# An encoder kernel on one Trainium2 core: the triangular inverses of its RWKV chunks by substitution in blocks of 16 and small products

## The chip, the cores and the metric

The kernel runs on one core of one Trainium2 chip. The metric is the time of one execution in microseconds (us) on the device. The engines' names in the profile are PE (TensorE, matrix products), PEld (its weight loads), DVE (VectorE), ACT (ScalarE), POOL (GpSimd) and SP (SyncE, which here issues transfers).

## What is computed

Two requests of 512 and 256 rows go through two layers of width 1024. Layer 0 runs differential attention and a bidirectional RWKV-7 mixer side by side, layer 1 runs dilated attention, and each layer ends with a SwiGLU feed-forward part. The change touches the RWKV mixer alone, whose recurrence is, for each of 8 heads of width 64, once forward and once backward in time:

```python
def step(st, inp):
    r_t, w_t, k_t, v_t, kk_t, a_t = inp
    sa = jnp.einsum('bhvk,bhk->bhv', st, -kk_t)
    st = (st * w_t[:, :, None, :] + sa[..., None] * (kk_t * a_t)[:, :, None, :]
          + v_t[..., None] * k_t[:, :, None, :])
    y = jnp.einsum('bhvk,bhk->bhv', st, r_t)
    return st, y
...
y = (rwkv_scan(rh, heads(decay(w0_f, w1_f, w2_f)), heads(k_f), vh, kk, heads(a_f), False)
     + rwkv_scan(rh, heads(decay(w0_b, w1_b, w2_b)), heads(k_b), vh, kk, heads(a_b), True))
```

The kernel computes it in chunks of 64 rows. The rows of a chunk depend on one another through a triangular 64 x 64 matrix, one for each head, chunk and direction, and the kernel needs its inverse.

## The kernel before

The program has one long stage for each part of the network. What follows concerns the stretch from about 185 to 400 us, in which the operands of the RWKV mixer are made. Its loop runs over four steps j, one for each pair of heads; each step projects r, k and v (TensorE, tiles `gm`), and then does for the forward and the backward direction: `stage` (small products into `st` and `uv`, sigmoids `sw` and `sa` on ScalarE, L670), `operands` (a scan of `sw` on VectorE, exponentials `E` and `sw` on ScalarE, and passes of 768 columns on VectorE that make `kff` or `kfb`, `AL`, `RH`, `KB`, `KK`, L593 to L607), `store` (transfers), and `products` (64 x 64 products `pr<-AL,KB` on TensorE, L83, which ScalarE copies out of the accumulation banks in strips, L643 into `G`, L646 into `AO`). `G` collects the two 32 x 32 diagonal blocks of each chunk's matrix, `AO` the block off the diagonal. A group is 16 of the 48 pairs of chunk and step, with both heads and both directions on the 128 partitions in quarters of 32.

As soon as a group is full, `inverses` calls `invert` (L721): after step 1, 2 and 3 for group 0, 1 and 2. It transposes `G` into `M` (L728, L729), sets `X` to the identity, and finds the inverse of the 32 x 32 blocks by substitution, row by row, on VectorE:

```python
for i in range(1, 32):
    o = 0
    for k0, k1 in zip(KI, KI[1:]):
        if k0 < i:
            row(i, k0, min(i, k1), o)
        o += (31 - k0) * (k1 - k0)
```

A row is a product (L736) and a sum (L738), in two strips of columns (`KI`), 48 pairs for a group. Four transposes then bring the inverse into `M` and `tm` (L749, L750), twelve copies into `TS`, `Tif` and `Tib` (L768; eight on ScalarE, four on GpSimd), 64 products of 32 x 32 join the blocks over `AO` (`iv<-TS,AO`), a copy `Hs` (L773) and 64 more products follow (`iv<-Tif,Hs`, `iv<-Tib,Hs`), and ScalarE copies the result and issues its transfer to DRAM (L785). It is read only by the later RWKV stage, whose chain starts near 485 us.

The order of all instructions is planned when the program is built, by a scheduler that simulates the engines and takes the row with the best rank that is ready; products with `fp32r` operands, the `gm` rows, rank last and fill gaps. A change in one function so moves rows of others, and each engine then runs its rows in the planned order.

Of the kernel before, what the change touches and what calls it, by code (L numbers as in the profile page):

```python
# [8 lines left out]
F32 = mybir.dt.float32  # L9
# [4 lines left out]
ALU = mybir.AluOpType  # L14
AX = mybir.AxisListType
# [3 lines left out]
P = 128  # L19
# [11 lines left out]
NF = FH // P  # L31
SEQS = ((0, 512), (512, 256))
RT = 2
KI = (0, 14, 32)
SUBS = [lambda nc: nc.vector, lambda nc: nc.gpsimd] * 2
DUPS = [lambda nc: nc.scalar.copy] * 2
SPLIT = ((0, 512), (512, 256))
# [10 lines left out]
COLS, NCOL = {}, 0  # L48
# [5 lines left out]
class Core:  # L54
# [13 lines left out]

    def constants(self):
        for n, shp in (("ident", [P, P]), ("cols", [P, NCOL]), ("blk2", [P, 2]), ("nblk", [2, P])):  # L70
            t = self.const.tile(shp, F32, tag=n, name=n)
            self.nc.scalar.dma_start(t, self.A[n])
            setattr(self, n, t)

    def rank(self, n):

        return self.tc.high_priority(n)
# [643 lines left out]
    def invert(self, g, G, AO, park):  # L721

        nc = self.nc
        tile = lambda tag, shape: self.ip.tile(shape, F32, tag=tag, name=self.uid(tag), bufs=1)
        M, X, tm = tile("M", [P, 32, 32]), tile("X", [P, 32, 32]), tile("tm", [P, 32 * 32])
        nc.vector.transpose(out=M[0:64], in_=G[0:64])  # L728
        nc.vector.transpose(out=M[64:P, ::-1, ::-1], in_=G[64:P])  # L729
        nc.gpsimd.memset(X, 0.0)  # L730
        nc.gpsimd.memset(X.rearrange("p a b -> p (a b)")[:, ::33], 1.0)

        def row(i, k0, k1, o):
            n, w = k1 - k0, i - k0
            tv = tm[:, o:o + n * w].rearrange("p (a b) -> p a b", a=n)
            nc.vector.tensor_tensor(out=tv, in0=X[:, k0:k1, k0:i],  # L736
                                    in1=M[:, i, k0:i].unsqueeze(1).to_broadcast([P, n, w]), op=ALU.mult)
            nc.vector.tensor_reduce(out=X[:, k0:k1, i], in_=tv, axis=AX.X, op=ALU.add)  # L738
        for i in range(1, 32):

            o = 0
            for k0, k1 in zip(KI, KI[1:]):
                if k0 < i:
                    row(i, k0, min(i, k1), o)
                o += (31 - k0) * (k1 - k0)
        TN, TT = M, tm.rearrange("p (a b) -> p a b", a=32)
        for h, rv in ((slice(0, 64), False), (slice(64, P), True)):
            xv = X[h, ::-1, ::-1] if rv else X[h]
            nc.vector.transpose(out=TN[h], in_=xv)  # L749
            nc.vector.transpose(out=TT[h], in_=xv.rearrange("p j i -> p i j"))  # L750
        TS, Hs = tile("TS", [P, 16, 32]), tile("Hs", [P, 16, 32])
        Ti = [tile(n, [P, 16, 64]) for n in ("Tif", "Tib")]
        parts, copies = [], []
        for di in range(2):
            for par in range(2):
                q = 64 * di + 32 * par
                ba = di
                bb = 1 - ba
                ra, rb = (slice(64 * par + 32 * x, 64 * par + 32 * x + 32) for x in (ba, bb))
                tc = "p t c -> p c t"  # L760
                nc.gpsimd.memset(Ti[di][rb, :, 32 * ba:32 * ba + 32], 0.0)
                copies.append((TS[ra], TN[q:q + 32, :, 16 * ba:16 * ba + 16].rearrange(tc)))
                for x, rr in ((ba, ra), (bb, rb)):
                    copies.append((Ti[di][rr, :, 32 * x:32 * x + 32], TT[q:q + 32, :, 16 * x:16 * x + 16].rearrange(tc)))
                parts.append((di, ba, bb, ra, rb))

        for i, (o, x) in enumerate(copies):
            (nc.gpsimd.tensor_copy if i % 3 == 2 else nc.scalar.copy)(out=o, in_=x)  # L768
        hb = self.bank("iv")
        for c in range(16):  # L770
            for di, ba, bb, ra, rb in parts:
                self.mm(hb[rb, c * 32:c * 32 + 32], AO[ra, c], TS[ra, c])
        nc.scalar.copy(out=Hs.rearrange("p c t -> p (c t)"), in_=hb)  # L773
        hb = self.bank("iv")
        for c in range(16):
            for di, ba, bb, ra, rb in parts:
                self.mm(hb[ra, c * 32:c * 32 + 32], Hs[rb, c], Ti[di][rb, c, 32 * bb:32 * bb + 32])
        for di, ba, bb, ra, rb in parts:
            nc.scalar.copy(out=Ti[di][ra, :, 32 * bb:32 * bb + 32], in_=hb[ra].rearrange("p (c t) -> p c t", c=16))
        for di in range(2):  # L780
            s = 0
            while s < 16:
                j, c = divmod(16 * g + s, 12)
                n = min(16 - s, 12 - c)
                nc.scalar.dma_start(park["Ti"][di, c:c + n, :, j].rearrange("c p x -> p c x"), Ti[di][:, s:s + n])  # L785
                s += n
# [846 lines left out]
```

## Time and profile before

| what | us |
|---|---|
| three runs | 2128.83, 2131.68, 2135.7 (median 2131.68) |
| profiled execution, its own time | 2133.74 |
| span of its trace | 2131.9 |
| TensorE busy | 2032.7 (95%) |
| VectorE busy | 1372.7 (64%) |
| ScalarE busy | 889.9 (42%) |
| GpSimd busy | 784.8 (37%) |

The mean granted clock of TensorE over the span is 0.96 of its full level. In a timeline a row is one instruction (or several alike, xcount): its start and its duration in us, engine, line, operation, output and inputs, and in brackets the idle time of the engine before it with what ended it. TensorE's rows overlap at their ends, so the time that one takes of the engine is the distance from its start to the next one's.

### The profile page before, as it was taken

Reading aid. Unit: us, or ns where it says so; the run is one execution under the profiler, and the core shown is the slowest. Engines: PE = TensorE matmul, PEld = TensorE weight load, DVE = VectorE, ACT = ScalarE, POOL = GpSimd, SP = SyncE. Lnnn points to the kernel's source line nnn. Section 1 sums busy time; section 2 is a strip of 40 time slices with the busy share of each in tenths; the row PEclk is TensorE's granted clock in tenths of the full one; section 3 lists DMA queues with packets and bytes.
Section 4 is the critical chain, followed back from the end, with each engine's and each line's share of the span. In section 5 each row is a group of like instructions: output and inputs, shape, how many; then the busy total and the mean of one; then the engine's idle time right before and its main releaser. Section 6 shows DMA issues by size and latency. Waiting matters only on the chain. (4 is left out here: it accounts for less than half of the span.)

```text
span 2131.9 us, 33719 instructions
## 1 busy us (share of the span) xinstructions
PE 2032.7 (95%) x13270; PEld 1758.0 (82%) x13270; DVE 1372.7 (64%) x2211; ACT 889.9 (42%) x1670; POOL 784.8 (37%) x783
## 2 busy tenths in 40 slices
PE   7998888999998989999999999999998999999998
PEld 7776564777877778999999998988678999999997
DVE  6457896756578567566666667544566566666665
ACT  4465644547544254433333334222454433333332
POOL 2000110642123157534435535443137544543442
PEclk9998886989999999999999999999999999999999
DMA  4333334304355312211221236121131122221124
GB/s 155 95 77 89 73 79 129 93 22 131 100 173 151 125 62 66 79 60 60 79 79 60 79 129 205 62 70 49 40 114 55 63 87 70 69 70 60 60 80 148
DMA packets 150227, 189.01 MB, mean 89 GB/s; under 512 B 95926, under 2 KB 107784, under 8 KB 150068
## 3 DMA queue, kind: packets, MB, share of 16 engines
q1 hardware_dynamic: 126880, 168.00, 25.3%
q10 hardware_dynamic: 20372, 12.03, 2.0%
q0 software_dynamic: 2816, 6.83, 1.0%
q8 instruction: 104, 1.70, 0.3%
q14 instruction: 55, 0.45, 0.1%
HBM read 150.20 MB, written 36.23 MB: 87 GB/s over the span
## 5 line engine op out<-in xcount | busy, mean ns | idle before, releaser
L82 PE MATMUL gm<-xh,w 128*128 128x384 f32 x896 | 249.0, 342 | 2.9 <-ACT xh L138 2.9
L82 PE MATMUL gm<-xh,wh 128*128 128x256 f32 (+3 forms) x640 | 211.2, 348 | 4.7 <-ACT hg L488 4.7
L139 DVE TENSOR_TENSOR wl<-wraw,wh 128x1024 fp32r<-128x1024 f32 (+1 forms) x96 | 120.8, 1259 | 146.1 <-ACT wh L138 146.0
L82 PE MATMUL gm<-xl,wh 128*128 128x256 f32 (+3 forms) x640 | 209.4, 346 | 0.0
L82 PE MATMUL gm<-T,w 128*128 128x384 f32 x1032 | 203.3, 339 | 5.6 <-ACT w L138 5.5
L82 PE MATMUL gm<-xh,wl 128*128 128x256 f32 (+3 forms) x640 | 208.4, 346 | 0.0
L139 DVE TENSOR_TENSOR w<-S,w 128x512 fp32r<-128x512 f32 x176 | 169.6, 965 | 44.3 <-ACT w L138 36.7
L82 PEld LDWEIGHTS gm<-T,w 128*128 128x128 f32 x1032 | 183.7, 188 | 10.9 <-ACT w L138 7.2
L138 ACT CAST wh<-wraw 128x1024 fp32r<-128x1024 f32 (+1 forms) x103 | 107.5, 1045 | 192.6 <-PE gm L82 125.3
L82 PEld LDWEIGHTS gm<-xh,w 128*128 128x128 f32 x896 | 167.6, 192 | 8.0 <-ACT xh L138 3.7
L138 ACT CAST w<-S 128x512 fp32r<-128x512 f32 x176 | 109.1, 621 | 153.5 <-POOL S L290 54.4
L138 ACT CAST w<-wraw 128x512 fp32r<-128x512 f32 x126 | 75.8, 620 | 207.9 <-PE gm L82 138.5
L82 PE MATMUL gm<-xl,w 128*128 128x384 f32 x448 | 153.6, 343 | 3.6 <-DVE xl L139 3.6
L82 PEld LDWEIGHTS gm<-xh,wh 128*128 128x128 f32 (+1 forms) x640 | 121.0, 194 | 28.8 <-issue 8.2
L139 DVE TENSOR_TENSOR w<-wraw,w 128x512 fp32r<-128x512 f32 x126 | 117.4, 948 | 39.4 <-ACT w L138 39.2
L82 PE MATMUL sc<-xh,w 128*128 128x384 f32 x512 | 140.9, 336 | 1.7 <-DVE u L329 1.1
L292 POOL TENSOR_TENSOR S<-wraw,S 128x512 f32<-128x512 f32 x42 | 62.9, 1497 | 205.2 <-DVE w L139 205.2
L82 PEld LDWEIGHTS gm<-xl,wh 128*128 128x128 f32 (+1 forms) x640 | 120.6, 194 | 19.2 <-issue 7.2
L82 PEld LDWEIGHTS gm<-xh,wl 128*128 128x128 f32 (+1 forms) x640 | 120.3, 193 | 18.4 <-issue 5.0
L391 DVE TENSOR_TENSOR acc<-acc,ob 128x512 f32<-128x512 f32 x128 | 87.5, 684 | 65.6 <-PE ob L82 64.5
L82 PE MATMUL sc<-T,w 128*128 128x384 f32 x552 | 113.7, 346 | 8.0 <-ACT v L349 3.5
L82 PE MATMUL ob<-wl,hh 128*128 128x512 f32 x288 | 113.4, 394 | 0.0
(499 smaller groups left out, 5088.6 us busy)
## 6 DMA issues: line engine op xcount, KB each, us to landing
wraw<-in_gate SPq DMA_DIRECT2D x44, 512.0 KB, 3.4
wraw<-in_down SPq DMA_DIRECT2D x44, 512.0 KB, 3.7
wraw<-in_up SPq DMA_DIRECT2D x40, 512.0 KB, 3.4
wraw<-in_wqk SPq DMA_DIRECT2D x20, 512.0 KB, 3.9
wraw<-in_wo SPq DMA_DIRECT2D x14, 512.0 KB, 4.1
wraw<-in_wrkv SPq DMA_DIRECT2D x12, 512.0 KB, 3.6
KB<-pkKB SPq DMA_DIRECT2D x24, 256.0 KB, 3.5
pkx<-x SPq DMA_DIRECT2D x12, 512.0 KB, 3.2
```

The source lines that it names most:

```text
L82: return self.nc.tensor.matmul(o, a, b, start=start, stop=stop)
L138: self.nc.scalar.copy(out=hi, in_=x)
L139: (eng or self.nc.vector).tensor_tensor(out=lo, in0=x, in1=hi.bitcast(F32), op=ALU.subtract)
L292: eng.tensor_tensor(out=s2, in0=a12, in1=s2, op=ALU.subtract)
L391: nc.vector.tensor_tensor(out=accs[t][:, fs], in0=accs[t][:, fs], in1=os[t, f], op=ALU.add)
```

## The change

The substitution now runs over 15 rows instead of 31, on both 16 x 16 diagonal blocks of each 32 x 32 block at once (one product and one sum for a row, L744 and L745, 30 instructions for a group). After the four transposes, new code fills the block of 16 x 16 that is left: a first round of 128 products of 32 x 16 (`iv<-M,G`), a copy `X<-iv` on ScalarE (L759), a second round of 64 (`iv<-X,tm`), two passes on VectorE that add the result into `M` under a mask of rows (L767), a third round of 128 (`iv<-tm,X`), and two passes that add into `tm` (L776). Each product is two instructions on TensorE. Operands of the products are read with a step of 32 elements where the diff indexes the last dimension (`TN[q, halves[di], c]`, `G[q, :, c]`, `TT[q, :, b]`, `TT[q, halves[1 - di], c]`). The mask is made at the start, by four sums over `ident`. The rest of `invert`, from `TS` on, is as it was, at L795 to L812.

```diff
-KI = (0, 14, 32)
...
-            t = self.const.tile(shp, F32, tag=n, name=n)
-            self.nc.scalar.dma_start(t, self.A[n])
+            t = self.const.tile([shp[0], shp[1] + 2 * (n == "cols")], F32, tag=n, name=n)
+            self.nc.scalar.dma_start(t[:, 0:shp[1]], self.A[n])
             setattr(self, n, t)
+
+        self.rows16 = m = self.cols[:, NCOL:NCOL + 2]
+        for di, h in enumerate((slice(0, 64), slice(64, P))):
+            for x in range(2):
+                o = 16 * (di ^ x)
+                self.nc.vector.tensor_reduce(out=m[h, x:x + 1], in_=self.ident[h].rearrange("p (a b) -> p a b", b=32)[:, :, o:o + 16],
+                                             axis=AX.XY, op=ALU.add)
...
-        def row(i, k0, k1, o):
-            n, w = k1 - k0, i - k0
-            tv = tm[:, o:o + n * w].rearrange("p (a b) -> p a b", a=n)
-            nc.vector.tensor_tensor(out=tv, in0=X[:, k0:k1, k0:i],
-                                    in1=M[:, i, k0:i].unsqueeze(1).to_broadcast([P, n, w]), op=ALU.mult)
-            nc.vector.tensor_reduce(out=X[:, k0:k1, i], in_=tv, axis=AX.X, op=ALU.add)
-        for i in range(1, 32):
-
-            o = 0
-            for k0, k1 in zip(KI, KI[1:]):
-                if k0 < i:
-                    row(i, k0, min(i, k1), o)
-                o += (31 - k0) * (k1 - k0)
+        def both(x, *dims):
+
+            return bass.AP(x.tensor, x.offset, [x.ap[0], [16 * 33, 2], *dims])
+        for i in range(1, 16):
+            tv = tm[:, 0:2 * i * i].rearrange("p (h a b) -> p h a b", h=2, a=i)
+            nc.vector.tensor_tensor(out=tv, in0=both(X[:, 0, 0:1], [32, i], [1, i]), in1=both(M[:, i, 0:1], [0, i], [1, i]), op=ALU.mult)
+            nc.vector.tensor_reduce(out=both(X[:, 0, i:i + 1], [32, i]), in_=tv, axis=AX.X, op=ALU.add)
...
+        quads = [(di, slice(64 * di + 32 * par, 64 * di + 32 * par + 32)) for di in range(2) for par in range(2)]
+        halves = (slice(0, 16), slice(16, 32))
+        Hx = X.rearrange("p a b -> p (a b)")
+        hb = self.bank("iv")
+        for c in range(32):
+            for di, q in quads:
+                self.mm(hb[q, c * 16:c * 16 + 16], G[q, :, c], TN[q, halves[di], c])
+        nc.scalar.copy(out=Hx[:, 16:528], in_=hb)
+        hb = self.bank("iv")
+        for c in range(16):
+            for di, q in quads:
+                b = 16 * di + c
+                self.mm(hb[q, c * 16:c * 16 + 16], TT[q, :, b], Hx[q, 16 + 16 * b:32 + 16 * b])
+        for di, h in enumerate((slice(0, 64), slice(64, P))):
+            o = TN[h, halves[di], 16 * di:16 * di + 16]
+            nc.vector.scalar_tensor_tensor(out=o, in0=hb[h, 0:256].rearrange("p (c n) -> p n c", c=16), scalar=self.rows16[h, 1:2], in1=o,
+                                           op0=ALU.mult, op1=ALU.add)
+        hb = self.bank("iv")
+        for c in range(32):
+            for di, q in quads:
+                s = 16 * c + 16 * (1 - di)
+                self.mm(hb[q, c * 16:c * 16 + 16], Hx[q, s:s + 32], TT[q, halves[1 - di], c])
+        for di, h in enumerate((slice(0, 64), slice(64, P))):
+            o = TT[h, halves[1 - di]]
+            nc.vector.scalar_tensor_tensor(out=o, in0=hb[h].rearrange("p (c n) -> p n c", c=32), scalar=self.rows16[h, 0:1], in1=o,
+                                           op0=ALU.mult, op1=ALU.add)
```

Since the scheduler plans anew, the order moves too. Two places follow, in step 2 (the third), around the backward direction. A row is a line, an operation and its tiles with their numbers; xN stands for N such rows in succession.

On ScalarE before, the two halves of the sigmoid `sa_1957` come ahead of the exponential `E_1970`:

```order
L670 ACTIVATE sa_1957<-uv_1959,cols 128x512
L643 COPY G_1249<-pr_1910 32x6x32
...
L670 ACTIVATE sw_1956<-st_1964,cols 128x256
L670 ACTIVATE sa_1957<-uv_1965,cols 128x256
L594 ACT_TABLE_LOAD
L594 ACTIVATE E_1970<-sw_1956 128x768
```

On ScalarE now (the same two halves are `sa_2223`, the exponential `E_2236`):

```order
L676 ACTIVATE sa_2223<-uv_2225,cols 128x512
L676 ACTIVATE sw_2222<-st_2230,cols 128x256
L600 ACT_TABLE_LOAD
L600 ACTIVATE E_2236<-sw_2222 128x768
L601 ACTIVATE sw_2222<-sw_2222 128x768
L795 COPY Tif_1740<-tm_1371 32x16x32 x2
L795 COPY Tib_1741<-tm_1371 32x16x32 x2
L649 COPY G_1253<-pr_2195 32x2x32
...
L676 ACT_TABLE_LOAD
L676 ACTIVATE sa_2223<-uv_2231,cols 128x256
```

The second half of `sa` moved behind `E`, `sw`, the four copies `Tif` and `Tib`, twelve copies into `G` and `AO` and a second table load; the four copies `TS_1738` of group 0 also moved up, ahead of the first half. Before, all copies of group 0 stood behind that step's backward products.

On TensorE before, both halves of the backward `uv` stand ahead of or close behind the first forward `pr`, and no small product of group 0 ahead of the backward `pr_1998`:

```order
L83 MATMUL uv_1959<-ha,a_485 128x512
...
L83 MATMUL pr_1910<-AL_1890,KB_1892 64x64 x12
L83 MATMUL st_1964<-hw,w_484 128x256
L83 MATMUL uv_1965<-ha,a_485 128x256
...
L83 MATMUL pr_1929<-AL_1890,KB_1892 64x64 x12
...
L83 MATMUL pr_1998<-AL_1976,KB_1978 64x64 x12
```

On TensorE now (the backward `uv` are `uv_2225` and `uv_2231`, the backward `pr` is `pr_2264`):

```order
L89 MATMUL iv_1540<-X_1370,tm_1371 32x16 x64
L89 MATMUL pr_2176<-AL_2156,KB_2158 64x64 x12
L89 MATMUL uv_2225<-ha,a_489 128x512
...
L89 MATMUL iv_1607<-tm_1371,X_1370 32x16 x128
L89 MATMUL pr_2195<-AL_2156,KB_2158 64x64 x12
L89 MATMUL uv_2231<-ha,a_489 128x256
...
L89 MATMUL iv_1758<-TS_1738,AO_852 32x32 x64
...
L89 MATMUL pr_2264<-AL_2242,KB_2244 64x64 x12
```

The three new rounds of group 0 and the first old one now stand ahead of `pr_2264`, and the second half of the backward `uv` moved behind the second forward `pr`. Counted over the whole order, 887 `gm` rows of the program stand ahead of `pr_1998` before and 857 ahead of `pr_2264` now; ahead of the forward `uv` of the last step (its second half) it is 1029 `gm` rows and 128 small products before, and 999 and 640 now.

## Rows read from the trace of the kernel before

**Rows 1.** The page, part 1: busy us (share of the span) and instructions.
```profile
PE 2032.7 (95%) x13270; PEld 1758.0 (82%) x13270; DVE 1372.7 (64%) x2211; ACT 889.9 (42%) x1670; POOL 784.8 (37%) x783
```

**Rows 2.** Windows: start:end, length, busy us (x instructions) of PE, PEld, DVE, ACT, POOL, PEclk, DMA.
```profile
220.00:240.00 20.00, 17.60 (x118) 12.61 (x116) 19.28 (x34) 9.99 (x21) 0.00 (x0) 0.84 0.29 68
240.00:260.00 20.00, 16.08 (x113) 11.98 (x114) 19.61 (x26) 14.96 (x27) 9.96 (x6) 0.83 0.42 99
260.00:280.00 20.00, 17.55 (x306) 11.82 (x306) 14.96 (x64) 15.21 (x27) 0.58 (x2) 0.76 0.32 77
300.00:320.00 20.00, 14.23 (x90) 8.64 (x89) 19.13 (x22) 12.15 (x22) 5.93 (x6) 0.87 0.21 40
320.00:340.00 20.00, 11.86 (x284) 6.81 (x284) 6.87 (x9) 12.15 (x18) 0.93 (x2) 0.59 0.64 140
340.00:360.00 20.00, 18.56 (x54) 8.87 (x55) 15.20 (x75) 6.47 (x15) 1.73 (x4) 0.50 0.32 92
```

**Rows 3.** Groups by line, VectorE, 185 to 400 us: busy us, mean ns.
```profile
L736 DVE TENSOR_TENSOR tm<-X,M 128x1 f32<-128x1 f32 (+15 forms) x144 | 44.0, 334 | 1.0
L738 DVE TENSOR_REDUCE X<-tm 128x1 f32<-128x1 f32 (+15 forms) x144 | 43.2, 329 | 1.0
L750 DVE STREAM_TRANSPOSE tm<-X 64x1024 f32<-64x1024 f32 x6 | 11.7, 1958 | 0.0
L749 DVE STREAM_TRANSPOSE M<-X 64x1024 f32<-64x1024 f32 x6 | 7.4, 1236 | 0.1
```

**Rows 4.** Timeline of VectorE, third group: start, us, line, operation.
```profile
358.31 0.41 DVE L736 TENSOR_TENSOR tm<-X,M 128x252 f32<-128x252 f32 x1
358.76 0.42 DVE L738 TENSOR_REDUCE X<-tm 128x14 f32<-128x252 f32 x1
378.94 0.58 DVE L736 TENSOR_TENSOR tm<-X,M 128x406 f32<-128x406 f32 x1
```

**Rows 5.** Timelines of TensorE: the small products, and one limited by weight loads.
```profile
203.76 1.39 PE L83 MATMUL pr<-rk,kfb 128*128 128x2 f32 x12
...
264.78 1.24 PE L83 MATMUL iv<-TS,AO 32*32 32x32 f32 x122
```

**Rows 6.** Groups by line, ScalarE, 185 to 420 us.
```profile
L768 ACT COPY TS<-M 32x512 f32<-32x512 f32 x12 | 13.0, 1085 | 0.8 <-DVE M L749 0.5
L773 ACT COPY Hs<-iv 128x512 f32<-128x512 f32 x3 | 1.7, 573 | 0.0
```

**Rows 7.** Timeline of ScalarE, third step, backward direction.
```profile
234.73 0.47 ACT L670 ACTIVATE sa<-uv,cols 128x256 f32<-128x256 f32 x1
235.22 1.28 ACT L594 ACT_TABLE_LOAD   x1
238.94 0.25 ACT L643 COPY G<-pr 32x64 f32<-32x64 f32 x1
242.19 0.86 ACT L488 COPY hg<-gm 128x512 f32<-128x512 f32 x2
```

**Rows 8.** Timelines of VectorE and TensorE, same place.
```profile
243.58 0.95 DVE L601 TENSOR_TENSOR KB<-sa,sw 128x768 f32<-128x768 f32 x1
...
248.85 0.39 PE L82 MATMUL gm<-xh,wh 128*128 128x512 f32 x1
249.08 0.39 PE L82 MATMUL gm<-xl,wh 128*128 128x512 f32 x1
249.88 0.91 PE L83 MATMUL pr<-AL,KB 64*64 64x64 f32 x24
```

**Rows 9.** Timelines of TensorE, VectorE, ScalarE: the last step, 299 to 345 us.
```profile
299.78 0.38 PE L83 MATMUL uv<-ha,a 64*128 64x256 f32 x1
...
309.32 1.24 DVE L749 STREAM_TRANSPOSE M<-X 64x1024 f32<-64x1024 f32 x1
344.63 1.24 DVE L729 STREAM_TRANSPOSE M<-G 64x1024 f32<-64x1024 f32 x1 [12.56 <-ACT G L643]
...
338.32 0.95 ACT L643 COPY G<-pr 32x192 f32<-32x192 f32 x2 [5.63 <-issue]
```

## The prediction

> **What bounds the kernel now.** I read the page first: TensorE is busy 95% of the span, VectorE 64% [rows 1]. Work taken from VectorE can shorten the kernel only where TensorE waits for it, and work given to TensorE costs its full time wherever TensorE is the one that never waits. So the second view is the table of windows over the stretch that the change touches [rows 2]. The reader is to see three things there. From 220 to 260 us VectorE is nearly full (19.28 and 19.61 of 20), and TensorE busy 17.60 and 16.08 at granted clocks of .84 and .83. From 300 to 345 us TensorE has its largest hole: 14.23 and 11.86 busy of 20, the clock down to .59; VectorE is full in the first half of it and nearly idle in the second. From 340 us TensorE is busy 18.56 of 20 at .50, the lower of its two levels, so there it sets the pace again. Taking busy time times clock as work done, TensorE loses 18.6 us of the 60 from 220 to 280 (5.2, 6.7, 6.7) and 20.6 of the 40 from 300 to 340 (7.6, 13.0). These 39 us are all that a lighter VectorE could ever give back. The third view, the timelines, says what ends the waits.
>
> **The change part by part.**
>
> *Substitution.* Before, products and sums take 44.0 + 43.2 us for three groups [rows 3], 29.1 us a group. One instruction takes .41 us at 252 elements and .58 at 406, that is 1.10 ns an element, and the next starts .45 us after the first [rows 4]: .17 + 1.10 ns times the elements. The new rows have 2 x 1240 elements in 15 products and the same in 15 sums: 30 x .17 + 4960 x 1.10 ns = 10.6 us. The four masked passes on VectorE, by the same law at 256 and 512 elements, are 2 x .45 + 2 x .73 = 2.4 us. VectorE is relieved of 29.1 - 13.0 = 16.1 us a group. The transposes stay, 2 x 1.236 + 2 x 1.958 = 6.4 us a group [rows 3].
>
> *Products.* 320 products are added to a group, 640 TensorE instructions. The nearest row is the present small product: 122 in 1.24 us, 10.2 ns each [rows 5]. 640 x 10.2 ns = 6.5 us a group, which I take, since the new ones have the same 32 x 32 quarters. The low end comes from a row limited by its weight loads, 12 of 128 columns in 1.39 us: a quarter of 116 ns, four quarters side by side, 7.2 ns, so 4.6 us. The high end takes the dearer reading of a spaced operand: a ScalarE copy with a spaced input lasts 1085 ns, a plain one 573 [rows 6], a factor 1.9, so 12.4 us. [...]
>
> *ScalarE.* One copy of 573 ns a group is new [rows 6]; it does not touch the path by itself. What matters is the order.
>
> *Step 2, backward direction.* Before, the second half of `sa` starts at 234.73 us [rows 7], and `KB` ends at 243.58 + .95 = 244.5 [rows 8], well before TensorE reaches the backward `pr` at 249.88, for which it then does not wait. Now ahead of that half stand the copies `TS`, `Tif` and `Tib`, eight of 1.085 us [rows 6], 8.7 us; the table load and exponentials, at most 3.7 us (235.22 to 238.94); twelve strips into `G` and `AO`, 3.3 us (238.94 to 242.19); and a table load of 1.28 [rows 7]. That is up to 17 us, or 251.7 at the latest; ScalarE's queue was not full there, so I put `sa` at about 250. Behind it VectorE has five passes of .95 us [rows 8] and little else, since the substitution is over: `KB` ends near 255. TensorE reaches `pr` with 30 `gm` rows fewer done (512 columns take .23 us [rows 8], 256 half of that; mean some .18), -5.5 us, and 384 products or 768 instructions more, +7.8 us: at 252. It waits about 3 us, where the old order had no wait. From there to the forward `uv` of the last step both orders have 142 `gm` rows. At that `uv` the balance is: 30 `gm` rows fewer, now of the longer kind, 30 x .21 = -6.4; 512 products more, 1024 x 10.2 ns = +10.4; the wait, +3; less what is regained because the copies and products of group 0 no longer interrupt the window 260 to 280, which loses 6.7 us [rows 2]. Nothing regained gives +7, all of it about 0; I take **+3.5**.
>
> *Last step.* From that `uv` at 299.78 to the transpose at 344.63, which waits for the last strips of `G`, the chain is 44.8 us long [rows 9]. In it the four old transposes stand between the passes of the two directions (from 309.32 on, 6.2 us), and ScalarE's issue of the inverse's transfers delays the strips by 5.63 us [rows 9]. In the new order the transposes are done before the step begins, but the copies `TS`, `Tif` and `Tib` still stand ahead of the second half of `sa`, two masked passes take 1.5 us, and the issue of the transfers still stands before the last strips. Between 0 and -11.8 I take **-4**. The 57 `gm` rows that are left behind the `uv` (27 before) fit into the hole of the windows 300 to 340.
>
> *Group 2.* Its products come after 345 us, where TensorE waits for nothing: **+6.5** (4.6 to 12.4). The 16.1 us of VectorE go there without effect, because the inverse is read only much later.
>
> *Start.* Four sums of 64 elements, .24 us each by the law above, stand on VectorE ahead of the first normalised rows: **+.8** of about 1.0.
>
> *Sum.* 3.5 - 4 + 6.5 + .8 = +6.8 on the profiled 2133.74 gives 2140.5. That execution stands 2.1 us above the median of the runs, 2131.68, so the forecast is **2138 us**. With the terms at their ends it runs from 2125 to 2152.
>
> **The rivals.**
>
> *Spaced operands are dear (slower).* Every new product reads one operand with a step of 32 elements. [...] At the factor 1.9 group 2 adds 5.9 us more and the 1024 instructions ahead of the last step 9.4 more, of which I let half vanish in waits: 6.8 + 5.9 + 4.7 = +17.4, **2149 us**. It decides from about 13 ns a product on. [...]
>
> *VectorE was the bound (faster).* If the full windows 220 to 260 and 300 to 320 mean that TensorE loses its time to VectorE's queue, groups 0 and 1 return up to 2 x 16.1 of the 39 us lost. Two thirds, 21 us, against products of 10.4 - 6.4, group 2 and the start (4.0 + 6.5 + .8 = 11.3) gives -10, **2122 us**; all of it 2111, a third 2132. For it speak the counts of busy time. Against it speaks the order: ahead of the `KB` of step 2 VectorE had 20.1 us of the inverse before (29.1 less the transposes, 6.4, and the last two rows, 4 x .64), and has 10.6 + 6.4 + 2.4 = 19.4 now, so the relief lies behind the place where it is wanted; and in the hole's second half VectorE is idle.
>
> *Nothing shows.* The products of all three groups fit into waits, as group 0's now largely do, and the relief of VectorE is worth as little as I think: about +.8, **2132 us**. Against it speaks that from 345 us TensorE has hardly a wait to fill.
>
> **How the numbers follow.** A measurement of this kernel can tell about 0.3%, 6.4 us, from no change: 2125.3 to 2138.1 is the same. My forecast has .45, and its own range 2125 to 2152 lies across the upper bound: .02 faster, .25 same, .18 slower. Spaced operands have .15, slower. VectorE as the bound has .25, .22 faster and .03 same. Nothing shows has .15: .12 same, .03 faster. Sums: .27 faster, .40 same, .33 slower. The range 2118 to 2149 leaves out the better half of VectorE's case and the worse half of the spaced operands, with the tail of the forecast.
>
> **What would show it.** Right: the new `iv` rows near 10 ns an instruction; a wait of a few us ahead of the backward `pr` of step 2, ended by VectorE's `KB`; the last step's chain some 4 us shorter; TensorE's busy time in 345 to 400 us up by one group's products. Wrong: `iv` rows of 16 ns or more at full clock (spaced operands); the loss of TensorE in 220 to 280 and 300 to 340 cut by more than 12 us in all (VectorE was the bound); a wait of 8 us or more at that `pr`, which would mean that ScalarE's queue, not TensorE's, is the dear part.

## The result and the profile after

The changed kernel takes **2158.76 us** (2154.42 to 2161.72), the kernel before 2130.69 in the same comparison: a ratio of 1.0126 [1.0101, 1.0151], 28.1 us slower. The forecast, 2138 us with a range of 2118 to 2149, was too low by 20.8 us. The profiled execution took 2161.72 us, its span 2159.9.

The page of the changed kernel, part 1, beside [rows 1]:

```profile
PE 2052.5 (95%) x15190; PEld 1779.0 (82%) x15190; DVE 1326.5 (61%) x2029; ACT 893.8 (41%) x1675; POOL 784.1 (36%) x783
```

VectorE lost 46.2 us of busy time, TensorE gained 19.8 us and 1920 instructions, while the kernel became 28.1 us longer. So something is lost that is not TensorE's busy time. The windows, columns as in [rows 2]:

```profile
220.00:240.00 20.00, 17.99 (x474) 13.65 (x474) 10.07 (x15) 12.86 (x18) 2.17 (x3) 0.84 0.28 56
240.00:260.00 20.00, 11.57 (x326) 10.20 (x325) 12.36 (x17) 15.20 (x32) 6.05 (x5) 0.60 0.33 67
260.00:280.00 20.00, 17.75 (x88) 12.89 (x87) 11.97 (x34) 9.72 (x22) 2.07 (x4) 0.91 0.44 99
...
300.00:320.00 20.00, 18.03 (x383) 13.26 (x384) 6.48 (x9) 6.95 (x8) 0.00 (x0) 0.82 0.16 31
320.00:340.00 20.00, 18.37 (x410) 12.64 (x410) 6.14 (x10) 15.77 (x25) 5.33 (x6) 0.74 0.27 57
340.00:360.00 20.00, 17.49 (x89) 9.50 (x88) 7.80 (x15) 8.76 (x19) 2.66 (x5) 0.79 0.65 152
...
380.00:400.00 20.00, 15.84 (x600) 13.59 (x600) 4.71 (x6) 8.35 (x9) 0.00 (x0) 0.90 0.63 185
400.00:420.00 20.00, 17.25 (x387) 14.98 (x387) 5.76 (x10) 9.77 (x12) 11.05 (x9) 0.76 0.12 45
```

VectorE is full in none of them: 12.36 at most where it had 19.61. The hole of TensorE between 300 and 340 is filled. A new one stands at 240 to 260 (11.57 of 20 at .60). The last two windows were, before:

```profile
380.00:400.00 20.00, 18.68 (x220) 15.28 (x220) 17.69 (x24) 13.33 (x13) 14.12 (x12) 1.00 0.35 132
400.00:420.00 20.00, 20.00 (x222) 15.65 (x221) 11.72 (x23) 11.56 (x18) 15.12 (x15) 1.00 0.26 54
```

In these two TensorE now stands idle for 4.2 and 2.8 us, before 1.3 and none, and the granted clock, 1.00 in both before, is .90 and .76. The groups of TensorE from 185 to 425 us name the place (busy us, mean ns | idle us ahead of them and what ended it):

```profile
L89 PE MATMUL iv<-M,G 32*32 32x16 f32 x768 | 13.0, 206 | 6.5 <-issue 6.5
L89 PE MATMUL iv<-tm,X 32*32 32x16 f32 x768 | 8.7, 189 | 9.6 <-issue 9.6
L89 PE MATMUL iv<-X,tm 32*32 32x16 f32 x384 | 6.0, 203 | 0.0
```

These are rounds 1, 3 and 2 of the three groups. Their 1920 instructions (matmuls, as in the prediction; each has a weight load beside it) take 27.7 us, 14.4 ns each: 16.9 ns in round 1, 11.3 in round 3, 15.6 in round 2. On top, 16.1 us stand idle inside rounds 1 and 3, ended by "issue": TensorE waits there for nothing that the profile shows. The timeline of the third group shows where (start, us, line, operation; in brackets the idle time before):

```profile
380.10 3.28 PE L89 MATMUL iv<-M,G 32*32 32x16 f32 x216
385.29 0.76 PE L89 MATMUL iv<-M,G 32*32 32x16 f32 x36 [1.91 <-issue]
...
386.56 0.63 PE L88 MATMUL gm<-wh,xh 128*128 128x512 f32 x1
...
389.19 2.00 PE L89 MATMUL iv<-X,tm 32*32 32x16 f32 x128
...
395.99 1.75 PE L89 MATMUL iv<-tm,X 32*32 32x16 f32 x186
402.75 1.15 PE L89 MATMUL iv<-tm,X 32*32 32x16 f32 x70 [5.00 <-issue]
```

The two rounds of 256 instructions break off after 220 (4 stand some rows ahead) and after 186 of them, stand for 1.91 and 5.00 us and go on; round 2, 128 instructions long, has no gap. Ahead of the gaps, at the full clock, round 1 takes 15.2 ns an instruction (3.28 us for 216) and round 3 takes 9.4; the means above hold the slower rest behind the gaps too. All six long rounds of the kernel have such a gap: .87, 2.01, 3.71, 2.59, 1.91 and 5.00 us. After the first gap shown, a `gm` row of 512 columns takes .63 us instead of .39 or .40, at a granted clock of .50. Beside each of the six the clock goes from 1.00 to .50 for 3.4 to 10.2 us; that the gaps cost it is my reading, and in two of the six it falls .4 and .7 us ahead of the gap.

The page lists a DMA queue `q8` of the kind "instruction": 104 packets before, 119 now, of 16 KB. Matmuls and weight loads together are 2 x 13270 and 2 x 15190, which is 255 a packet in both. By that count, an estimate, a packet stands for some 128 matmuls with their loads, 1.4 to 2.2 us of a round's work. The DMA view around the last gap, first 397.8 to 400.2 us, then 400.2 to 401.4 (packets, MB, share of 16 engines):

```profile
q1 hardware_dynamic: 431, 0.87, 98.1%
...
q1 hardware_dynamic: 89, 0.17, 37.0%
q8 instruction: 1, 0.02, 5.5%
```

While the data queue kept the engines 98.1% busy, no instruction packet came; one came when it had drained, and TensorE went on at 402.75. Each of the six gaps ends 1.4 to 1.6 us after such a packet has landed. The trace shows one thing more. Count TensorE's instructions in the order of their start: matmuls, weight loads and the 207 of its sequencer. The instruction with which a round goes on is then, in all six, number 193 or 194 of a block of 256 (near the 255 a packet, 257 with the sequencer's), and so it is at a seventh stop of .48 us (259.68 us, behind a row of 151 small instructions). All seven stops come at the same place of a block. From that place one block earlier the rounds need 1.3 to 2.1 us to use the block up, and TensorE goes on only after 2.9 to 6.3 us. In two of the six the 16 DMA engines carried no data after the block's start, and the next packet began .56 and .83 us behind it; in the other four data kept them 82 to 96% busy, and it began 1.5 to 3.8 us behind. So I read the gaps as **TensorE using up its instructions faster than they are supplied**. This is a reading: the trace gives the packets' size and times, not what they hold.

### The profile page after: what moved, and what is told of

The parts are those of the page before. It is cut to its first block, busy times and chain, and to the rows that moved or that the text cites. A ratio compares the mean times of both kernels' runs of the same rounds, so it can differ in the third digit from the quotient of the medians.

```text
span 2159.9 us, 37368 instructions
## 1 busy us (share of the span) xinstructions
PE 2052.5 (95%) x15190; PEld 1779.0 (82%) x15190; DVE 1326.5 (61%) x2029; ACT 893.8 (41%) x1675; POOL 784.1 (36%) x783
## 5 line engine op out<-in xcount | busy, mean ns | idle before, releaser
L88 PE MATMUL gm<-xh,wh 128*128 128x256 f32 (+3 forms) x640 | 206.0, 344 | 0.0
L88 PE MATMUL gm<-xl,wh 128*128 128x256 f32 (+3 forms) x640 | 204.7, 344 | 0.0
L88 PE MATMUL gm<-xh,wl 128*128 128x256 f32 (+3 forms) x640 | 203.6, 343 | 0.0
L88 PEld LDWEIGHTS gm<-T,w 128*128 128x128 f32 x1032 | 184.6, 189 | 12.8 <-ACT w L144 8.6
L145 DVE TENSOR_TENSOR w<-wraw,w 128x512 fp32r<-128x512 f32 x126 | 113.6, 918 | 44.8 <-ACT w L144 44.6
```

Source lines behind the costliest of these rows:

```text
L88: return self.nc.tensor.matmul(o, a, b, start=start, stop=stop)
L145: (eng or self.nc.vector).tensor_tensor(out=lo, in0=x, in1=hi.bitcast(F32), op=ALU.subtract)
```

## The experiments

All ratios are to the kernel before. The theory was: spaced weights, gaps in the supply, and prices that add. In the expectations F stands for it, P for the price of the products alone, O for the new order on ScalarE, L for the luck of a new plan.

**Rounds 1 and 3 direction by direction.** Each half uses a bank turn of its own, so that 128 instructions stand in a row.

```
+        for dd in range(2):
+            hb = self.bank("iv")
             for c in range(32):
-                for di, q in quads:
+                for di, q in quads[2 * dd:2 * dd + 2]:
                     self.mm(hb[q, c * 16:c * 16 + 16], G[q, :, c], TN[q, halves[di], c])
+            nc.scalar.copy(out=Hx[hs[dd], 16:528], in_=hb[hs[dd]])
```

> The first and the third new round are made direction by direction, each half with its own turn of the accumulation bank, so no more than 64 products (128 instructions) follow one another; the sums are the same. Theory F (in a run of 256 small instructions TensorE outruns the arrival of its own instructions: six gaps of 0.9 to 5.0 us, 16 us, and half clock behind them): the gaps vanish, 2138 to 2145 us. Rival P (only the price of the products themselves, 15 ns and not 10, counts): as after the change, 2155 to 2162. Rival O (the new order on ScalarE counts): the same 2155 to 2162.

Measured: 2145.55 us, 1.0066 [1.0044, 1.0089], 13.2 us less than the change, just above the range expected. The same groups:

```profile
L89 PE MATMUL iv<-M,G 32*32 32x16 f32 x768 | 23.1, 206 | 0.0
L89 PE MATMUL iv<-tm,X 32*32 32x16 f32 x768 | 13.2, 183 | 0.0
```

The gaps are gone. But a half's instructions go to only two of the four 32 x 32 quarters, and an instruction of round 1 takes 30 ns instead of 16.9, one of round 3 17 instead of 11.3. Counted, that is 14.6 us more instructions and 16.1 us of gaps less, a gain of some 2; 13.2 were measured. What the rest comes from is open.

**Near weights.** Rounds 1 and 2 load their weights from neighbouring elements; the order is identical.

```
-                self.mm(hb[q, c * 16:c * 16 + 16], G[q, :, c], TN[q, halves[di], c])
+                self.mm(hb[q, c * 16:c * 16 + 16], G[q, c, :], TN[q, halves[di], c])
...
-                self.mm(hb[q, c * 16:c * 16 + 16], TT[q, :, b], Hx[q, 16 + 16 * b:32 + 16 * b])
+                self.mm(hb[q, c * 16:c * 16 + 16], TT[q, b, :], Hx[q, 16 + 16 * b:32 + 16 * b])
```

> The weights of the first and second round are read from neighbouring elements (this takes other elements, so the inverses come out wrong); the planned order is the same. Rival P: 15.5 ns become 9.5 in 384 instructions a group, 2.3 us a group, 7 us in all: 2150 to 2153. Theory F: the second round gains 0.8 us a group, but in the first the gap grows as the instructions run out sooner: 2154 to 2158. Rival O: no change.

Measured: 2155.57 us, 1.0113 [1.0087, 1.0139], 3.2 us less than the change; the two intervals overlap, so the time alone shows no gain. The rows do:

```profile
L89 PE MATMUL iv<-M,G 32*32 32x16 f32 x768 | 8.9, 188 | 8.1 <-issue 8.1
L89 PE MATMUL iv<-X,tm 32*32 32x16 f32 x384 | 4.1, 182 | 0.0
L89 PE MATMUL iv<-tm,X 32*32 32x16 f32 x768 | 8.7, 189 | 9.9 <-issue 9.9
```

Spacing costs 6.0 us of instructions: 16.9 to 11.6 ns in round 1, 15.6 to 10.7 in round 2. Round 3, whose weights are near and whose moving operand is spaced, had 11.3 ns already, and in this run round 1, with a spaced moving operand, is no slower at full clock (2.04 us for 221) than round 2 with both near (1.26 for 128): here spacing is dear for the weights and free for what moves. The faster rounds wait longer, though (gaps 18.0 against 16.1), as they would if the supply sets the pace.

**No rounds at all.** The three rounds, the copy of their result and the masked passes are left out.

> The three new rounds, the copy X and the four masked passes are left out (the inverses lack the block off the diagonal of each 32 x 32 block); what stays is the halved substitution on VectorE. Theory F and rival P: the 27 us of products, the 16 us of gaps and the half clock behind them go, and 2115 to 2128 remains, at or below before. Rival O: half or less of the loss goes, 2140 or more.

Measured: 2115.52 us, 0.9921 [0.9895, 0.9947]. This splits the change in two. VectorE's relief, with the new order, is worth **14.9 us** (the kernel before took 2130.45 in this comparison; by the interval 11 to 22). The rounds, with their copy, their masked passes and the order that they bring, cost **43.2 us**, beside 27.7 of instructions and 16.1 of gaps, 43.8 together. The two runs are known to some 8 us between them, and the lower clock beside the gaps is in neither figure, so the close agreement is partly chance; that in this kernel the rounds cost about their full time is not.

**The kernel before, with the rounds added.** Their result is multiplied by a mask of zeros, so that they are work alone.

```
+        self.rows16 = self.const.tile([P, 2], F32, tag="rows16", name="rows16")
+        nc.gpsimd.memset(self.rows16, 0.0)
...
+        hb = self.bank("iv")
+        for c in range(32):
+            for di, q in quads:
+                self.mm(hb[q, c * 16:c * 16 + 16], G[q, :, c], TN[q, halves[di], c])
...
```

> The kernel before, with the three rounds, the copy X and the four passes added under a mask of zeros (they change nothing); VectorE keeps all 31 rows of the substitution. Theory F and rival P: the whole loss and more, 2155 to 2175, with gaps in the rounds of 256 and none in those of 128. Rival O: 2140 or less, since VectorE's substitution holds the copies of the group back as before.

Measured: 2146.38 us, 1.0072 [1.0049, 1.0094], 16 us more than before where I expected at least 25.

```profile
L85 PE MATMUL iv<-M,G 32*32 32x16 f32 x768 | 12.8, 207 | 2.8 <-issue 2.8
L85 PE MATMUL iv<-tm,X 32*32 32x16 f32 x768 | 8.3, 188 | 7.4 <-issue 7.4
```

The instructions cost the same 27 us and there are 10.2 us of gaps, in five of the six long rounds, yet the time grows by less than half of it. The likely reason, argued only, is that TensorE still waits for VectorE there and the rounds fall into those waits. So the prices do not add: the rounds cost 16 us with the long substitution and 43 without it.

**Rounds 1 and 3 cut by columns.** All four quarters are used throughout, but in rows of 128 instructions, each with a bank and a copy (or a masked pass on 16 columns) of its own.

```
+        for ch in range(2):
             hb = self.bank("iv")
-            for c in range(32):
+            for c in range(16):
                 for di, q in quads:
-                    self.mm(hb[q, c * 16:c * 16 + 16], G[q, :, c], TN[q, halves[di], c])
-            nc.scalar.copy(out=Hx[:, 16:528], in_=hb)
+                    self.mm(hb[q, c * 16:c * 16 + 16], G[q, :, 16 * ch + c], TN[q, halves[di], 16 * ch + c])
+            nc.scalar.copy(out=Hx[:, 16 + 256 * ch:272 + 256 * ch], in_=hb[:, 0:256])
```

> The first and the third round are cut by columns instead: 64 products on all four quarters, then the bank is emptied, then the other 64; the sums are the same. No run of small instructions is longer than 128, and four quarters work at once, unlike in the cut by direction, where an instruction of the first round took 30 ns. Theory F: no gaps, 640 instructions at 9 to 16 ns, 8 us a group: 2124 to 2138 us, faster than the cut by direction by about the 15 us that this spends on half-filled quarters. Rival P: 2150 or more. Rival L (the gain of the cut by direction was luck of the new plan): anywhere, with no relation to gaps.

Measured: 2145.94 us, 1.0073 [1.0053, 1.0093].

```profile
L89 PE MATMUL iv<-M,G 32*32 32x16 f32 x768 | 13.0, 204 | 0.4 <-ACT X L760 0.4
L89 PE MATMUL iv<-tm,X 32*32 32x16 f32 x768 | 8.0, 184 | 0.0
L89 PE MATMUL iv<-X,tm 32*32 32x16 f32 x384 | 6.0, 203 | 0.0
L89 PE MATMUL iv<-TS,AO 32*32 32x32 f32 x384 | 4.1, 193 | 1.4 <-issue 1.4
```

The same instructions at the same price and no "issue" gap in the rounds: 12.8 us less than the change. This is the cleanest run on the gaps: **the length of the row, not the number of instructions, makes them.** One stop of 1.35 us is left, in a row of 128 instructions `iv<-TS,AO` at 255.89 us, again at number 193 of a block. There the block held two `gm` rows and 126 of the small instructions and was used up in 1.7 us; in this run the shortest block that holds part of a round took 2.2 us. So the pace at which a block of 256 is used up seems to count, but not alone: in the change a block with most of a row of 128 `iv<-TS,AO` is used up in 1.5 us from 331.51 on, without a stop; two packets had landed during the block ahead of it. The size was missed (2124 to 2138 expected): 16.1 us of gaps return as 12.8, and the cut by direction, with 14.6 us more of instructions, is as fast, which stays unexplained.

**No rounds in the third group.** An `if g < 2:` stands around the three rounds.

> The three rounds are left out for group 2 alone (its inverses lack the block off the diagonal); groups 0 and 1 keep them. Theory F: in the last group, where TensorE waits for nothing else, they cost 9 us of instructions, 7 of gaps and about 4 of half clock: 2159 - 20 = 2135 to 2143. If only the instructions count there: 2149 to 2152.

Measured: 2149.59 us, 1.0091 [1.0059, 1.0124], 9.2 us less than the change, where 16 to 24 were expected. That equals the instructions of one group (9.2 us) without its gaps. But the four runs scatter from 2141.50 to 2157.24, and the two intervals allow anything from nothing to some 16 us, so this run does not tell whether the gaps' share came back.

**Only a new plan.** The order is computed anew when line counts change. Two kernels keep the old substitution of the kernel before and move only its first strip border (14 to 15, and to 13).

```
+KI = (0, 15, 32)
```

> The kernel before, with the first strip of the substitution 15 instead of 14 columns wide: the work on VectorE hardly differs (under 1 us a group), but the whole order is planned anew. Rival L (a new plan alone moves the time by 10 us or more): outside 2122 to 2139. Theory F: 2124 to 2137.

> The same with 13 columns. Rival L: outside 2122 to 2139. Theory F: 2124 to 2137.

Measured: 2128.98 us, 1.0001 [0.9983, 1.0018], and 2129.82 us, 0.9997 [0.9982, 1.0011]. A slightly different plan by itself moves nothing here, which speaks against the 28 us being its chance.

**The copies on GpSimd.** In step 2 the changed kernel waits long for `KB` (below). ScalarE's copies `TS`, `Tif` and `Tib` of the first two groups go to GpSimd, eight a group; four were there already.

```
-            (nc.gpsimd.tensor_copy if i % 3 == 2 else nc.scalar.copy)(out=o, in_=x)
+            (nc.gpsimd.tensor_copy if i % 3 == 2 or g < 2 else nc.scalar.copy)(out=o, in_=x)
```

> The kernel after the change with all twelve copies of groups 0 and 1 on GpSimd, so ScalarE's queue is 8.7 us a group shorter ahead of the backward sigmoid. Theory F + O (besides instructions and gaps, ScalarE's queue costs the 8 us that TensorE waits ahead of the backward products of step 2): 2148 to 2155 us, with that wait under 4 us. Theory F alone: 2156 to 2162.

> The cut by columns with the same copies on GpSimd; here both halves of the backward sigmoid come ahead of the exponential again. Theory F + O: 2146 less 4 to 8, 2136 to 2142 us. Theory F alone: 2143 to 2149.

Measured: alone 2159.93 us, 1.0142 [1.0120, 1.0163], no change; with the rounds cut by columns 2128.76 us, 0.9997 [0.9983, 1.0011], 30 us less than the change and level with the kernel before. The first agrees with theory F alone; the second is faster than either expectation (2136 to 2142 and 2143 to 2149). The timeline of TensorE in the first shows why it gained nothing:

```profile
234.82 1.94 PE L89 MATMUL iv<-tm,X 32*32 32x16 f32 x209
238.85 0.61 PE L89 MATMUL iv<-tm,X 32*32 32x16 f32 x28 [2.08 <-issue]
...
240.86 1.22 PE L89 MATMUL uv<-ha,a 64*128 64x256 f32 x2
...
253.60 1.54 PE L89 MATMUL pr<-AL,KB 64*64 64x64 f32 x24 [4.61 <-DVE KB L607]
```

The second half of `uv` stands behind round 3, its gap and the forward `pr`, and ahead of `sa` ScalarE still has the strips of that `pr` and a table load, so `sa` starts at 245.59, only 2.0 us earlier than in the change. Even these are lost again on VectorE, while GpSimd runs the copies:

```profile
245.92 5.85 POOL L795 COPY Tib<-tm 32x512 f32<-32x512 f32 x4
...
250.79 1.80 DVE L613 TENSOR_TENSOR KK<-kfb,sw 128x768 f32<-128x768 f32 x1
252.51 0.94 DVE L607 TENSOR_TENSOR KB<-sa,sw 128x768 f32<-128x768 f32 x1
```

The copies on GpSimd end at 251.77. The passes that VectorE makes beside them last up to 1.80 us, the one behind them .94; in the change, where GpSimd is idle at that place, the pass for `KK` takes .95. So `KB` ends at 253.45, 1.1 us later than in the change. In the second kernel `sa` starts 14 us earlier than in the change:

```profile
233.48 0.47 ACT L676 ACTIVATE sa<-uv,cols 128x256 f32<-128x256 f32 x1
```

**A mixture.** As the kernel just shown, with the third group's inverse by the old substitution of 31 rows.

> The kernel of the cut by columns with the copies on GpSimd, but group 2 goes back to the substitution over 31 rows without rounds, since VectorE has room there and TensorE has none. Theory F: the 9 us of instructions of group 2 go, 2129 - 9 = 2116 to 2124 us, faster than both kernels. If group 2's rounds fitted into waits: 2126 to 2132.

Measured: 2130.51 us, 1.0009 [0.9992, 1.0025]. Taking the rounds out of the place where TensorE never waits brought nothing; the expectation of 2116 to 2124 fell, and why is open. Two "issue" stops, .80 and 1.64 us, stand in its 32 x 32 products, where the kernel just shown has none; that is a small part.

**The control: the kernel before with the copies on GpSimd**, and nothing else.

> The control for the last two: the kernel before with the twelve copies of groups 0 and 1 on GpSimd and nothing else. If the copies alone bring the gain, 2110 to 2122 us; theory F, by which VectorE's substitution still stands ahead of the passes there, 2125 to 2136.

Measured: **2119.22 us**, 0.9957 [0.9940, 0.9974]: faster than both kernels, inside the range for the copies alone and outside that of theory F. Its second half of `sa` and its hole, windows as in [rows 2]:

```profile
231.09 0.47 ACT L670 ACTIVATE sa<-uv,cols 128x256 f32<-128x256 f32 x1
```

```profile
300.00:320.00 20.00, 17.61 (x91) 7.02 (x89) 18.82 (x30) 13.59 (x29) 0.92 (x1) 0.59 0.64 149
320.00:340.00 20.00, 18.39 (x169) 10.36 (x169) 8.51 (x23) 5.42 (x11) 13.28 (x15) 0.66 0.34 117
340.00:360.00 20.00, 20.00 (x221) 16.61 (x221) 14.20 (x55) 8.84 (x12) 2.07 (x4) 1.00 0.66 195
```

Busy time times clock is 42.5 us in these 60, where it was 28.7 [rows 2], with VectorE nearly as full as ever from 300 to 320 (18.82). So a good part of that hole goes when the copies leave ScalarE's queue, though VectorE's work stays. The control also sets the level for the kernel with cut rounds and moved copies: against this base the block substitution, without a gap, still loses 9.5 us.

## Why the prediction was wrong

**The step that failed** is the term "640 x 10.2 ns = 6.5 us a group", with its bounds of 4.6 to 12.4. Measured: 640 x 14.4 ns = 9.2 us of instructions and 5.4 of gaps, 14.6 a group, above the high end. The instructions alone lay inside the bounds. The gaps lay outside because the row that I called nearest [rows 5] is a run of 122 instructions between other work; it has the same quarters but not the length of row, and rounds of 256 have a cost that no row of before could show. Nothing in the text asked how many such instructions stand one behind the other. The low bound took the quarters as working side by side and a small load as a quarter of a large one. The first agrees with the cut by direction (30 ns an instruction with two quarters, 16.9 with four); the second no run shows, and the cheapest row of a round, 9.2 ns an instruction (near weights), lies above its 7.2. The range was too narrow besides: its upper end took the high price, 12.4, for group 2 alone. The same price for the 1024 instructions ahead of the last step is 9.4 us more, and 2152 becomes 2161; that would have covered the measured time, but by dear instructions and not by gaps.

Put into the forecast's own sum, the price explains the miss in size. Of the new instructions 1024 + 640 were counted: 1664 x (14.4 - 10.2) ns = +7.0. The gaps in these two places are .87 + 2.01 + 3.71 and 1.91 + 5.00, +13.5. That gives 2138 + 20.5 = 2158.5, where 2158.76 was measured. The agreement is better than its parts, since other terms were off by some us and cancel:

- **Substitution.** Forecast 10.6 us a group of products and sums and 2.4 of masked passes. VectorE's groups, beside [rows 3]:

```profile
L744 DVE TENSOR_TENSOR tm<-X,M 128x2 f32<-128x2 f32 (+14 forms) x45 | 14.8, 329 | 1.3
L745 DVE TENSOR_REDUCE X<-tm 128x2 f32<-128x2 f32 (+14 forms) x45 | 14.6, 325 | 1.2
...
L776 DVE SCALAR_TENSOR_TENSOR tm<-iv,cols,tm 64x512 f32<-64x512 f32 x6 | 4.5, 750 | 14.9 <-PE iv L89 14.7
L767 DVE SCALAR_TENSOR_TENSOR M<-iv,cols,M 64x256 f32<-64x256 f32 x6 | 2.9, 482 | 15.2 <-PE iv L89 15.0
```

  (14.8 + 14.6) / 3 = 9.8 and (4.5 + 2.9) / 3 = 2.5: right. The idle columns show the price of alternating: 30 us in which VectorE waits for the rounds.
- **Step 2.** Forecast: `sa` at 250, `KB` at 255, a wait of 3 us ahead of `pr`. ScalarE, VectorE and TensorE, beside [rows 7, 8]:

```profile
247.60 0.47 ACT L676 ACTIVATE sa<-uv,cols 128x256 f32<-128x256 f32 x1
...
251.43 0.95 DVE L607 TENSOR_TENSOR KB<-sa,sw 128x768 f32<-128x768 f32 x1
...
248.12 1.01 PE L89 MATMUL uv<-blk,sq 128*128 128x2 f32 x4 [4.55 <-ACT sa L676]
252.53 1.54 PE L89 MATMUL pr<-AL,KB 64*64 64x64 f32 x24 [3.39 <-DVE KB L607]
```

  The chain and its place were right, and `KB` is 2.6 us earlier than forecast; but TensorE, whose queue reached that point earlier too, waits twice, 7.9 us instead of 3, the first time at a row that I had passed over. This wait stands in the new hole from 240 to 260. The forward `uv` of the last step comes at 311.30 instead of 299.78 [rows 9], +11.5 against the +3.5 forecast, although TensorE enters the stage 4.3 us earlier (`pr` at 199.46, before 203.76 [rows 5]).
- **Last step.** From there to the transpose that waits for the last strips of `G` it is 43.3 us, before 44.8: -1.5 against -4.

```profile
311.30 0.70 PE L89 MATMUL uv<-ha,a 64*128 64x256 f32 x2
...
354.58 1.24 DVE L735 STREAM_TRANSPOSE M<-G 64x1024 f32<-64x1024 f32 x1 [9.21 <-ACT G L649]
```

- **Group 2.** The last step's lag was 9.95 us (first `pr`, 346.25 before, 356.20 now); the first `sc` behind the group comes at 404.90 before and 430.66 now, 25.8 later. The group cost 15.8 us against 6.5: 9.2 of instructions, 6.9 of gaps. That nothing covers it was right. The other 2.2 us of the 28.0 between the two spans arise behind this place and were not followed.
- **Start.** The first normalised rows were forecast .8 later and are .3 later; the four sums went beside the wait for the constants.

**The rivals.** *Spaced operands are dear* was right on the weights, by 6.0 us in all, and came nearest in time (2149 against 2158.76), but the gaps, 16.1 us, weigh more, and it knew nothing of them. Its sign, 16 ns at full clock, was just missed (15.2 in round 1), and round 1 reads both operands with a step, not one as the prediction says. *VectorE was the bound* is partly true: leaving the rounds out shows that its relief is worth 14.9 us. Without its product terms (3.5 - 10.4 - 4 + .8) my sum would be 2121.5 us, beside 2115.52 measured, so the forecast had valued the relief 6 us too low. The rounds cost nearly three times as much. *Nothing shows* fell: rounds that fit into waits are seen only beside the old, long substitution, and even there the kernel gets 16 us longer.

That the gaps are the instruction supply rests on the length of row (present at 256, gone from the rounds at 128 with the same instructions), on the packets, and on the place of these stops in the blocks of 256; no run changed the supply itself. That data transfers delay the packet fits four of the six gaps, the longest among them; the other two came with the data queue idle. Why 16.1 us of gaps return as 12.8 stays open.

## What to carry to other kernels

Before pricing many tiny instructions by a row of the trace, see that the row has as many of them standing one behind the other; here rows of 256 at 11 to 17 ns each stopped for .87 to 5.00 us, by my reading for want of instructions, and cutting the row into halves, most of them with other work between, gave back 12.8 us. Let the weights be the operand that lies near (11.6 ns an instruction here, spaced 16.9), and spread a row over all four quarters (16.9 ns, over two 30). When a change moves copies and waits along with its arithmetic, run the old arithmetic with the moved copies as a control: here that control was the fastest of the kernels that compute the whole inverse, 10 us faster than the kernel before in the same comparison (2129.33).

## What the runs showed of the hardware

- All six rounds of 256 small matmuls in the change stop for .87 to 5.00 us at "issue", each at the same place of a block of 256 instructions (number 193 or 194), and go on 1.4 to 1.6 us after a 16 KB packet has landed on the instruction queue. No round of 128 stops, neither in the change (2.01 us for 128) nor in the two cuts into halves; in the cut by columns a row of 126 others that all but fills a block does, for 1.35 us, and in the change a row of 128 of the same others (1.29 us at 331.40) does not.
- A 32 x 32 product instruction of 16 columns (round 1) takes 16.9 ns on the mean with weights at a step of 32 elements and 11.6 with near ones (15.2 and 9.2 at full clock); a moving operand at the same step costs nothing measurable (9.2 ns an instruction beside 9.8 with both near, one row each).
- In rows that go to two quarters instead of four the same instruction takes 30 ns instead of 16.9 (round 1), 17 instead of 11.3 (round 3). Counted for one quarter, an instruction comes every 60 and 34 ns in rows over two, every 68 and 45 in rows over four.
- VectorE's passes of 768 columns, .95 us each, took up to 1.80 us while GpSimd ran copies (to 251.77 us, in the kernel where the copies alone are moved), and the one behind them, from 252.51 on, .94.
